# Two heads of sparse attention share one output bank and one transposed bank

## The chip, the core and the metric

The kernel runs on one core of one Trainium2 chip. The metric is the device time of one execution in microseconds (us), the median of several runs. TensorE (PE in the profile, PEld for its weight loads) multiplies, VectorE (DVE) and ScalarE (ACT) do the element work, GpSimd (POOL) and SyncE (SP) mainly issue transfers.

## The reference, cut to what matters

The program is a whole small network on 512 tokens of width 1024: two layers with a linear-recurrence mixer, sparse attention and a gated feed-forward stage, then a third layer with two further attentions, a cross attention and a mixture of 32 experts. The change is in the sparse attention of the first two layers (8 query heads of width 64, 2 key/value groups). Every head adds three attentions with a gate each:

```python
p_cmp = jax.nn.softmax(jnp.where(m_cmp, s, NEG), axis=-1) * m_cmp        # compressed keys
o_cmp = jnp.einsum('bghtn,bngd->btghd', p_cmp.astype(dt), vc)
...
pb = jax.nn.softmax(sb.reshape(B, G, Hg, SLC_QBLOCK, -1), axis=-1)       # selected blocks
return jnp.einsum('bghqns,bgqnsd->bghqd', pb.astype(dt), vg)
...
pw = jax.nn.softmax(jnp.where(mw, sw, NEG), axis=-1)                     # window
return jnp.einsum('bghqk,bkgd->bghqd', pw.astype(dt), vw)
...
o = (gate[..., 0:1] * o_cmp + gate[..., 1:2] * o_slc + gate[..., 2:3] * o_swa)
```

With 512 tokens there are 8 blocks and 16 may be selected, and the window is 512 wide, so the second and the third attention are both plain causal attention over all keys, with keys and values of their own.

## The kernel before, in words

Activations are held transposed, 128 features by 512 tokens to a tile. A product with weights is done in three matmuls of 128x512 (`mm3`, L284 to L286), since weights and activations are each split into a high and a low part. Weights come by `wload` (L266): a DMA on SP's queue into a tile `w`, then the split, ACT writing the high half `wh` (L260) and DVE the low half `wl` (L261). `w` has three buffers, `wh` and `wl` two each.

A layer is a list of steps, `ORDER`, and a list scheduler lays each engine's queue out from the order in which the steps are written and from their dependencies; splits of weights get a higher priority. P, L, A, O are the recurrence, V the values and inputs of the compressed branch, W the compression (96 matmuls of 64x256 with 8 weight tiles `in_c`), K and Q the keys and queries of a group or pair, C the compressed scores and probabilities of a group, H a head, R the two halves of the projection onto the residual. The half R0 needs the recurrence's output alone. Its 96 matmuls (tile `fmm`, weights `fw`, four loads with two buffers, the first held back by `fgate` until the norm of the layer is there) are a filler: the scheduler puts them wherever PE would have nothing else. The diff attention of the third layer uses the same filler lane with eight weight tiles.

A head (`nsa_head`, L801) writes rows 0 to 63 of one PSUM bank `O`. One matmul adds the compressed branch (L807). For each of the other two branches, the scores of the four query blocks (128 queries each, with 128, 256, 384 and 512 keys) come into banks `S` (L525, L526 and a mask, L530). For each block `softmax_rows` takes the row maximum on DVE (L546), a scale (L254), the exponential with row sum on ACT (L551), the reciprocal of the sum (L553), its product with the gate (L254) and the product of the rows with that (L627, by `by_row`), all but the exponential on DVE. `transposed` turns the block triangle of P, ten blocks of 128x128, in three groups of 512, 384 and 256+128 columns (L585, bank `PT`, one buffer) and copies each group to `pth`, every third copy on DVE (L594), the others on ACT (L596). `pv` (L624) adds values times `pth` to `O` with one matmul for each key block, of 512, 384, 256 and 128 columns, with 64 rows of output. The profile shows each of these matmuls as two instructions. At the end of a head ACT copies `O` (L638) and DVE subtracts (L639), for the split of the head's output.

The experts at the end of the program (L1538, L1559) use matmuls with 64 output rows too: neighbouring matmuls write alternately rows 0 to 63 and rows 64 to 127 of a bank.

Of the kernel before, what the change touches and what calls it, by code (L numbers as in the profile page):

```python
# [8 lines left out]
F32 = mybir.dt.float32  # L9
F32R = mybir.dt.float32r  # L10
# [6 lines left out]

PSUM_BUFS = dict(mm=3, fmm=2, tok=4, lev=4, S=3, PT=1, PU=2, O=1, X=2)
CAPS = dict(rT=2, m0=6, sb=1, nl=512, g0=5, w=3, wh=2, wl=2, tmp=6, lf=2, kk=2, qq=2, A=2, eu=3, kf=2, xc=2, rq=4, KH=4, KL=4, T=8, Pc=2,
            P=2, P2=2, pth=3, ptl=3, st=8, stc=2, r4=2, rsx=3, rsy=3, rst=3, hr=2, xtok=2, mh=8, ml=8,  # L20
            hh=22, hl=22, gt=10, sq=2, fw=2, fwh=2, fwl=2, yh=8, yl=8, mgh=8, mgl=8, MKH=4, MKL=4, yt=4, xt=4, ring=20, xgs=2, esg=2, eh=2, ex=2, ehT=2, ey=3, fs=4, fo=4)

ORDER = "P0 L0 A0 V0 O0 O1 W0 K0 Q0 Q1 C0 H0 H1 H2 H3 K1 Q2 Q3 C1 H4 H5 H6 H7 R0 R1"
# [208 lines left out]
class Net:  # L232
# [33 lines left out]
    def wload(self, ap, width, lane=""):  # L266

        nc = self.nc
        w = self.tile([128, 1024], F32, name=lane + "w")
        if lane and self.ngate < 2 * CAPS["fw"]:  # L270
            self.after(w, self.fgate)
            self.ngate += 1
        nc.sync.dma_start(w[:, :width], ap)
        wh = self.tile([128, 1024], F32R, name=lane + "wh")
        wl = self.tile([128, 1024], F32R, name=lane + "wl")
# [53 lines left out]
    def norm(self, src, gain, n=512, pfx="x", spread=True):  # L329
        nc = self.nc  # L330
        xh = self.tile([128, 8, n], F32R, name=pfx + "h")
        xl = self.tile([128, 8, n], F32R, name=pfx + "l")
        acc = self.tile([128, 512], F32, name="acc")
        for k in range(8):
            self.split(xh[:, k, :], xl[:, k, :], src[:, k, :], gain[:, k:k + 1])
            if k == 0:
                nc.scalar.activation(acc[:, :n], src[:, k, :], AF.Square)
            else:
                sq = self.tile([128, 512], F32, name="sq")
                nc.scalar.activation(sq[:, :n], src[:, k, :], AF.Square)  # L340
                self.tt(acc[:, :n], acc[:, :n], sq[:, :n], OP.add)
        nb = n // 128
        rt = self.column(nb)
        ps = self.mmT("X")
        self.sums(ps, acc[:, :n], self.c("ones")[:, 0:1], nb)
        self.rsqrt(rt, ps[:, :nb], 1.0 / D, 1e-6)
        rstd = None
        if spread:
            rstd = self.tile([128, n], F32, name=pfx + "rstd")
# [118 lines left out]
    def nsa_k(self, ps, gain, cos, sin, rtok):  # L468
# [11 lines left out]
        return self.k_stack(x)  # L480
# [9 lines left out]
    def q_stack(self, x, n=512):  # L490

        nc = self.nc
        t0 = self.tile([128, 512], F32R, name="T")
        t1 = self.tile([128, 512], F32R, name="T")
# [147 lines left out]
    def nsa_cv(self, l, xs, rstd, rtok):  # L642
# [11 lines left out]
        v = self.values(256, "nv", False)  # L654
# [24 lines left out]
    def compress(self, l, n):  # L679
# [73 lines left out]
        ckv = self.tile([128, 8, 64], F32, name="ckv")  # L753
# [47 lines left out]
    def nsa_head(self, l, n, h, hi, lo):  # L801

        nc = self.nc
        g = h // 4
        O = self.mmT("O")[:64]
        v = n["v"][0]
        nc.tensor.matmul(O, n["vc"][g][:, h % 4, :], n["pc"][g], start=True, stop=False)  # L807
        for br in range(2):
            Ps = self.p_tiles()
            self.softmax_rows(Ps, lambda qb, w: self.scores(n["q"][h], n["k"][br, g], qb, w, True), n["rq"][h],  # L810
                              n["gate"][:, :, h * 3 + 1 + br])
            pts = self.transposed(Ps, two=False)
            for kc in range(4):
                p, q0 = pts[kc]
                last = br == 1 and kc == 3
                self.pv(O[:, q0:], v[:, kc, br * 128 + g * 64:br * 128 + g * 64 + 64], p, False, last)
        self.out_heads(O, (h % 2) * 64, hi, lo)
# [150 lines left out]
    def layer1(self, l):  # L968
        nc = self.nc
        xs, rstd, rtok = self.norm(self.h, self.p(f"norm_mix{l}"))  # L970
        m = [[self.tile([128, 512], F32R, name=n) for n in ("mh", "ml")] for k in range(8)]
# [3 lines left out]
        def K(g):  # L975
            self.nsa_k_chunk(l, v["n"], xs, rtok, g)

# [6 lines left out]
        def H(h):  # L984
            self.nsa_head(l, v["n"], h, *m[4 + h // 2])
# [276 lines left out]
    def cross(self):  # L1262
# [5 lines left out]
        for i in range(CAPS["xgs"]):  # L1268
            t = self.tile([CAP, D], F32, name=f"xg{i}")
# [81 lines left out]
    def moe(self, out):  # L1351
# [149 lines left out]
        def slot():  # L1501
# [3 lines left out]
            if i < nring:  # L1505
                w = self.tile([128, 2048], F32, name=f"ring{i}")
# [143 lines left out]
def tile_net(ctx, tc, aps, out):  # L1650
# [5 lines left out]
    N.h = N.tile([128, 8, T], F32, name="h")  # L1656
    for k in range(8):
        nc.sync.dma_start(N.h[:, k, :], aps["xT"][:, k, :])
    N.nev = N.nrow = 0
    nc0, np0 = min(_CONST_COLS[n][0] for n in _EARLY), aps["par"].shape[1]  # L1660
    nc2 = aps["const"].shape[1] - nc0
    keep = N.tile([128, nc0 + np0 + 24 + 320 + 192], F32, name="const")
    early = N.tile([128, nc2 + 128 + 768 + 192], F32, name="const2")
# [65 lines left out]
```

## Time and profile before

| | us |
|---|---|
| median of 3 runs | 2526.38 |
| lowest and highest | 2524.33 and 2532.23 |
| the profiled execution, its own time | 2535.04 |
| its span in the profile | 2533.4 |
| PE busy | 2380.5 (94%) |
| DVE busy | 1353.9 (53%) |
| ACT busy | 968.1 (38%) |

The profile is read by stages. In time the stages are: layer one to 770 us, with its heads from about 243 to 400 us; layer two to 1500 us, with its heads from about 985 to 1145 us; the other attentions to about 1985 us; the experts and the tail to the end. The strip of the page that cuts the span into 40 slices shows one slice for each 63 us. "Busy" of PE counts matmul records, whose ends are modelled and overlap, so that a stretch can show 100% and still be packed tighter: what a group of matmuls takes of the engine's time is read from the start of one group to the start of the next.

### The profile page before, as it was taken

How to read it: one execution, taken by the hardware profiler on the slowest of the kernel's cores; microseconds unless marked ns; L12 is line 12 of the kernel's file. 1: busy time of each engine (PE TensorE's matmuls, PEld its weight loads, DVE VectorE, ACT ScalarE, POOL GpSimd, SP SyncE). 2: the span in 40 equal slices, each digit the busy share in tenths (PEclk: the TensorE clock that was granted, in tenths of full speed). 3: DMA queues.
4: the chain of work that ended last, by engine and by line, in shares of the span. 5: the costliest groups of instructions: out<-in, count | busy, mean ns of one | idle time of the engine just before them, and what ended most of it. 6: DMA issues, size and time to landing. Idle time of an engine off the chain costs nothing. (4 is left out here: it accounts for less than half of the span.)

```text
span 2533.4 us, 30397 instructions
## 1 busy us (share of the span) xinstructions
PE 2380.5 (94%) x11422; PEld 1679.7 (66%) x11423; DVE 1353.9 (53%) x3081; ACT 968.1 (38%) x1614; POOL 117.7 (5%) x180
## 2 busy tenths in 40 slices
PE   8999999999999999999999999999999798877776
PEld 6877558888888877558888887777788533222221
DVE  6788876444336778876444338867765511111112
ACT  6544554323226444554232226645443322111111
POOL 0000000000000000000000000000001111111110
PEclk9999999999999999999999999999999799999998
DMA  5123002333333132002333333132235699999997
GB/s 200 44 85 107 17 1 85 98 99 93 100 99 118 35 118 74 9 9 92 94 98 100 93 103 106 48 100 71 91 104 196 234 403 405 404 403 406 408 415 284
DMA packets 83448, 383.15 MB, mean 151 GB/s; under 512 B 12624, under 2 KB 13024, under 8 KB 57952
## 3 DMA queue, kind: packets, MB, share of 16 engines
q1 hardware_dynamic: 77312, 370.65, 41.2%
q0 software_dynamic: 5120, 8.40, 1.0%
q10 hardware_dynamic: 864, 2.10, 0.3%
q8 instruction: 91, 1.49, 0.3%
q14 instruction: 61, 0.50, 0.1%
HBM read 371.66 MB, written 12.59 MB: 152 GB/s over the span
## 5 line engine op out<-in xcount | busy, mean ns | idle before, releaser
L260 ACT ACTIVATE wh<-w 128x1024 fp32r<-128x1024 f32 (+1 forms) x264 | 276.5, 1048 | 615.2 <-PE mm L285 328.9
L284 PE MATMUL mm<-xh,wh 128*128 128x512 f32 x1232 | 490.3, 398 | 10.2 <-ACT wh L260 10.2
L285 PE MATMUL mm<-xl,wh 128*128 128x512 f32 x1232 | 486.2, 395 | 0.0
L286 PE MATMUL mm<-xh,wl 128*128 128x512 f32 x1232 | 484.4, 393 | 0.8 <-DVE wl L261 0.8
L261 DVE TENSOR_TENSOR wl<-w,wh 128x1024 fp32r<-128x1024 f32 (+1 forms) x264 | 320.0, 1212 | 172.8 <-ACT wh L260 171.5
L284 PEld LDWEIGHTS mm<-xh,wh 128*128 128x128 f32 x1232 | 232.7, 189 | 59.9 <-ACT wh L260 10.6
L285 PEld LDWEIGHTS mm<-xl,wh 128*128 128x128 f32 x1232 | 232.9, 189 | 48.2 <-issue 2.9
L286 PEld LDWEIGHTS mm<-xh,wl 128*128 128x128 f32 x1232 | 232.5, 189 | 48.3 <-DVE wl L261 1.4
L254 DVE TENSOR_TENSOR tmp<-mm,xrstd 128x512 f32<-128x512 f32 x104 | 71.7, 691 | 236.0 <-PE mm L286 229.6
L1538 PE MATMUL mm<-ring,ex 128*64 128x512 f32 x512 | 122.9, 613 | 33.2 <-DMA ring<-in_egu_dram 31.5
L1538 PE MATMUL fmm<-ring,ex 128*64 128x512 f32 x512 | 121.5, 606 | 32.4 <-DMA ring<-in_egu_dram 31.7
L284 PE MATMUL mm<-hh,wh 128*128 128x512 f32 x352 | 137.3, 390 | 0.0
L286 PE MATMUL mm<-hh,wl 128*128 128x512 f32 x352 | 137.2, 390 | 0.0
L285 PE MATMUL mm<-hl,wh 128*128 128x512 f32 x352 | 137.2, 390 | 0.0
L1559 PE MATMUL S<-ring,ehT 128*64 128x512 f32 x512 | 123.4, 605 | 12.9 <-DMA ring<-in_ed_dram 9.9
L1538 PEld LDWEIGHTS mm<-ring,ex 128*64 128x64 f32 x512 | 35.6, 139 | 119.1 <-issue 60.6
L1538 PEld LDWEIGHTS fmm<-ring,ex 128*64 128x64 f32 x512 | 35.2, 137 | 116.2 <-issue 60.2
L1525 ACT ACTIVATE xg<-xg,const 64x1024 f32<-64x1024 f32 x32 | 36.6, 1147 | 179.0 <-DMA xg<-x_d,const 179.0
L551 ACT ACTIVATE P<-S,st,const 128x128 f32<-128x128 f32 (+3 forms) x128 | 78.5, 616 | 52.8 <-DVE st L254 42.9
L254 DVE TENSOR_TENSOR eh<-fmm,esg 64x512 f32<-64x512 f32 x16 | 11.1, 693 | 163.3 <-ACT esg L1540 163.3
L254 DVE TENSOR_TENSOR eh<-mm,esg 64x512 f32<-64x512 f32 x16 | 11.1, 693 | 149.6 <-ACT esg L1540 149.5
L546 DVE TENSOR_REDUCE st<-S 128x1 f32<-128x128 f32 (+3 forms) x160 | 76.9, 485 | 26.0 <-PE S L530 25.0
(511 smaller groups left out, 4160.0 us busy)
## 6 DMA issues: line engine op xcount, KB each, us to landing
ring<-in_egu_dram SPq DMA_DIRECT2D x128, 1024.0 KB, 21.7
ring<-in_ed_dram SPq DMA_DIRECT2D x64, 1024.0 KB, 21.4
w<-in_fi_dram SPq DMA_DIRECT2D x88, 512.0 KB, 3.5
w<-in_w_dram SPq DMA_DIRECT2D x48, 512.0 KB, 4.1
w<-in_fo_dram SPq DMA_DIRECT2D x44, 512.0 KB, 3.6
w<-in_c_dram SPq DMA_DIRECT2D x16, 512.0 KB, 3.9
tmp<-tmp SPq DMA_DIRECT2D x80, 64.0 KB, 2.0
fw<-in_wo_dram SPq DMA_DIRECT2D x8, 512.0 KB, 4.6
```

Source lines behind the costliest of these rows:

```text
L254: (eng or self.nc.vector).tensor_tensor(out, a, b, op=op)
L260: nc.scalar.activation(hi, src, AF.Copy)
L261: nc.vector.tensor_tensor(lo, src, hi.bitcast(F32), op=OP.subtract)
L284: nc.tensor.matmul(ps, ah, bh, start=first, stop=False)
L285: nc.tensor.matmul(ps, ah, bl, start=False, stop=False)
L286: nc.tensor.matmul(ps, al, bh, start=False, stop=last)
L546: nc.vector.tensor_reduce(st[:, 0, i:i + 1], S[:, :n], axis=AX.X, op=OP.max, negate=True)
L551: nc.scalar.activation(Ps[q0 + i], S[:, :n], AF.Exp, bias=b, scale=1.0 if scale is None else scale[q0 + i], accum_out=st[:, 1, i:i + 1])
L1525: nc.scalar.activation(xg[:CAP], xg[:CAP], AF.Copy, scale=li_e[2])
L1538: nc.tensor.matmul(ps[r], x[:, k, :], w[:, at:at + 512], start=k == 0, stop=k == 7)
L1559: nc.tensor.matmul(py[r], hT[:, k, :], w[:, at:at + 512], start=k == 0, stop=k == 3)
```

## The change

Two heads go through `nsa_pair` together. Their outputs are rows 0 to 63 and 64 to 127 of one bank. For each branch there are five steps. Each fills one bank `PT` with 512 columns, half from each head, copies it to `pth` in one instruction on ACT, and adds it to `O` with matmuls of 64x256 (64x128 in the fifth step) that stand next to one another for the two heads. The reciprocal and the product with the gate are done once for four rows of statistics (two query blocks of two heads) instead of once for each. `PT` has two buffers instead of one. The output of a pair is copied and subtracted with 128 rows in one instruction each.

The space for this comes from elsewhere: `fw` has one buffer instead of two and waits for the keys of group 0 (`fgate` is set anew after K0); `pth`, `tmp`, `g`, `xc` and `ey` have one fewer; the constants, the residual `h` and a norm's `rstd` are one tile, over parts of which three expert weight buffers lie later; `w` and its halves are one tile each with places taken in turn (same depth).

```diff
-            P=2, P2=2, pth=3, ptl=3, st=8, ...
-            ... fw=2, ... ey=3, ...
+            P=4, P2=2, pth=2, ptl=3, st=8, ...
+            ... fw=1, ... ey=2, ...
-ORDER = "P0 L0 A0 V0 O0 O1 W0 K0 Q0 Q1 C0 H0 H1 H2 H3 K1 Q2 Q3 C1 H4 H5 H6 H7 R0 R1"
+ORDER = "P0 L0 A0 V0 O0 O1 W0 K0 Q0 Q1 C0 H0 H1 K1 Q2 Q3 C1 H2 H3 R0 R1"
-    def nsa_head(self, l, n, h, hi, lo):
...
-        nc.tensor.matmul(O, n["vc"][g][:, h % 4, :], n["pc"][g], start=True, stop=False)
+    def nsa_pair(self, l, n, c, hi, lo):
...
+        heads, rows = (2 * c, 2 * c + 1), (slice(0, 64), slice(64, 128))
+        for h, r in zip(heads, rows):
+            nc.tensor.matmul(O[r], n["vc"][g][:, h % 4, :], n["pc"][g], start=True, stop=False)
+
+        steps = (((0, 1), ((0, (0, 1)),)), ((2, 3), ((0, (2, 3)),)), ((), ((1, (2, 3)),)), ((), ((2, (2, 3)),)), ((), ((1, (1,)), (3, (3,)))))
         for br in range(2):
...
+            Ps = [self.p_tiles() for h in heads]
+            vs = slice(br * 128 + g * 64, br * 128 + g * 64 + 64)
+            for qbs, blocks in steps:
+                if qbs:
+                    st = self.tile([128, 4, 4], F32, name="st")
+                    for i, qb in enumerate(qbs):
+                        w = 128 * (qb + 1)
+                        for j, h in enumerate(heads):
+                            o, scale = slice(2 * j + i, 2 * j + i + 1), n["rq"][h][qb]
+                            S = self.scores(n["q"][h], n["k"][br, g], qb, w, True)
+                            nc.vector.tensor_reduce(st[:, 0, o], S[:, :w], axis=AX.X, op=OP.max, negate=True)
+                            self.tt(st[:, 3, o], st[:, 0, o], scale, OP.mult)
+                            nc.scalar.activation(Ps[j][qb], S[:, :w], AF.Exp, bias=st[:, 3, o], scale=scale, accum_out=st[:, 1, o])
+                    nc.vector.reciprocal(st[:, 2], st[:, 1])
...
+                    self.tt(r, r, gt, OP.mult)
+                    for i, qb in enumerate(qbs):
+                        for j in range(2):
+                            self.by_row(Ps[j][qb], st[:, 2, 2 * j + i:2 * j + i + 1])
+                pt = self.mmT(self.ptn)
...
+                            nc.tensor.transpose(pt[:, at:at + 128], Ps[j][qb][:, kc * 128:kc * 128 + 128], self.c("ident"))
...
+                p = self.tile([128, 512], F32, name="pth")
+                nc.scalar.activation(p, pt, AF.Copy)
+                for kc, j, qs, o in where:
+                    w = 128 * len(qs)
+                    nc.tensor.matmul(O[rows[j], qs[0] * 128:qs[0] * 128 + w], v[:, kc, vs], p[:, o:o + w],
+                                     start=False, stop=br == 1 and kc == 3)
+        nc.scalar.activation(hi, O, AF.Copy)
+        nc.vector.tensor_tensor(lo, O, hi.bitcast(F32), op=OP.subtract)
...
         def K(g):
             self.nsa_k_chunk(l, v["n"], xs, rtok, g)
+            if not g:
+                self.fgate = v["n"]["k"][0, 0][0].bitcast(F32)
```

On PE's queue, in the first layer, at the first values products of a branch, before: `O` is the output bank, `pth` the copied blocks, `nvh` the values, `KH`, `KL` and `T` keys and queries, `PT` the transposed bank.

```order
L585 MATMUL PT_2069<-const_70,P_2017 128x128 x3
L624 MATMUL O_2015<-pth_2067,nvh_996 64x512
L525 MATMUL S_2159<-KH_1759,T_1840 128x128
L526 MATMUL S_2159<-KL_1760,T_1840 128x128
L585 MATMUL PT_2075<-const_70,P_2017 128x128 x3
L624 MATMUL O_2015<-pth_2073,nvh_996 64x384
L530 LDWEIGHTS const2_71
L530 MATMUL S_2159<-const2_71 128x128
L624 MATMUL O_2015<-pth_2079,nvh_996 64x256
L624 MATMUL O_2015<-pth_2079,nvh_996 64x128
```

The same place now (`KK` is the stacked keys):

```order
L854 MATMUL O_1897<-pth_2004,nvh_941 64x256 x2
L854 MATMUL O_1897<-pth_2013,nvh_941 64x128 x4
L848 MATMUL PT_2056<-const_61,P_2019 128x128 x2
L848 MATMUL PT_2056<-const_61,P_2020 128x128 x2
L537 LDWEIGHTS const_61
L537 MATMUL S_2087<-const_61 128x128
L532 MATMUL S_2146<-KK_1652,T_1796 128x128
L533 MATMUL S_2146<-KK_1652,T_1796 128x128
L537 LDWEIGHTS const_61
L537 MATMUL S_2146<-const_61 128x128
L532 MATMUL S_2153<-KK_1652,T_1796 128x128
L854 MATMUL O_1897<-pth_2061,nvh_941 64x256 x2
```

The values products of one head, apart from one another and of unequal width, have become products of two heads that stand together with equal width.

On PE's queue at the end of the compression step W of the first layer, before: `xbh` and `xbl` are the inputs of the compression, the rows with `fmm` are the filler R0, and the rows with `mm<-xh` and `mm<-xl` begin the keys of group 0.

```order
L285 MATMUL mm<-wl,xbh 64x256
L286 MATMUL mm<-wh,xbl 64x256
L284 MATMUL mm<-xh,wh 128x512
L285 MATMUL mm<-xl,wh 128x512
L286 MATMUL fmm<-mh,fwl 128x512
L284 MATMUL fmm<-mh,fwh 128x512
L285 MATMUL fmm<-ml,fwh 128x512
L286 MATMUL mm<-xh,wl 128x512
```

And now (`wx` holds both halves of the weights):

```order
L292 MATMUL mm<-wx,xbh 64x256
L293 MATMUL mm<-wx,xbl 64x256
L291 MATMUL mm<-xh,wx 128x512
L292 MATMUL mm<-xl,wx 128x512
L293 MATMUL mm<-xh,wx 128x512
```

No filler stands here any more, nor among the compression's own 96 matmuls, where 20 stood before; the first `fmm` comes in the step C0.

On SP's queue of the first layer, before, while the recurrence's weights are loaded:

```order
L273 DMA w_410<-in_w3_dram 128x1024
L273 DMA fw_3474<-in_wo_dram 128x1024
L273 DMA fw_3509<-in_wo_dram 128x1024
L273 DMA fw_3544<-in_wo_dram 128x1024
L273 DMA w_446<-in_w3_dram 128x1024
L273 DMA fw_3579<-in_wo_dram 128x1024
```

Now, at the queries (the `tmp` transfers belong to the rotation of a pair's queries):

```order
L440 DMA tmp_1717<-tmp_1696 32x512
L441 DMA tmp_1717<-tmp_1696 32x512
L282 DMA fw_3194<-in_wo_dram 128x1024
L282 DMA w_179<-in_wo_dram 128x1024 x2
L440 DMA tmp_1787<-tmp_1766 32x512
L441 DMA tmp_1787<-tmp_1766 32x512
```

The four loads of `fw` have moved from the recurrence to behind the rotation of keys and of the first queries, and they stand apart, with other transfers queued behind each.

## Rows read from the trace of the kernel before

**Rows 1.** The page, busy tenths of 40 slices of the span.

```profile
PE   8999999999999999999999999999999798877776
DMA  5123002333333132002333333132235699999997
```

**Rows 2.** Stretches: busy us (count) of PE, PEld, DVE, ACT, POOL; PEclk, DMA share, GB/s.

```profile
243.00:400.00 157.00, 153.82 (x732) 92.71 (x731) 128.16 (x502) 86.58 (x208) 2.56 (x2) 1.00 0.06 18
985.00:1145.00 160.00, 156.27 (x741) 94.95 (x740) 127.75 (x518) 84.41 (x206) 2.56 (x2) 0.98 0.06 15
...
2100.00:2200.00 100.00, 82.30 (x415) 29.12 (x412) 12.67 (x21) 21.50 (x29) 13.01 (x14) 0.93 1.02 404
```

**Rows 3.** Timeline of PE in a head: start us, us, instruction, tile, count.

```profile
351.35 1.07 PE L624 MATMUL O<-pth,nvh 128*64 128x512 f32 x2
352.35 0.55 PE L585 MATMUL PT<-const,P 128*128 128x128 f32 x3
352.83 0.86 PE L624 MATMUL O<-pth,nvh 128*64 128x384 f32 x2
353.62 0.50 PE L526 MATMUL S<-KL,T 128*128 128x512 f32 x1
354.05 0.86 PE L624 MATMUL O<-pth,nvh 128*64 128x256 f32 x4
```

**Rows 4.** Timeline of PE at a head's compressed branch.

```profile
251.04 1.07 PE L807 MATMUL O<-pch,ckv 128*64 128x512 f32 x2
252.04 0.55 PE L585 MATMUL PT<-const,P 128*128 128x128 f32 x3
```

**Rows 5.** The experts on PE: timeline, and the group in 2100 to 2200 us (busy, mean ns).

```profile
2202.49 1.94 PE L1538 MATMUL mm<-ring,ex 128*64 128x512 f32 x8
...
L1538 PE MATMUL mm<-ring,ex 128*64 128x512 f32 x96 | 21.9, 597 | 4.2 <-DMA ring<-in_egu_dram 2.8 <-ACT ey L1562 1.3
```

**Rows 6.** Groups on DVE in 243 to 400 us: count, busy us, mean ns, idle before.

```profile
L254 DVE TENSOR_TENSOR st<-st,const 128x1 f32<-128x1 f32 x128 | 17.9, 158 | 0.7
L553 DVE RECIPROCAL st<-st 128x1 f32<-128x1 f32 x64 | 9.7, 158 | 6.1 <-ACT P L551 5.8
L594 DVE COPY pth<-PT 128x384 f32<-128x384 f32 x16 | 8.9, 557 | 6.9 <-PE PT L585 6.3
L627 DVE TENSOR_SCALAR P<-P,st 128x512 f32<-128x512 f32 x16 | 7.7, 482 | 0.2
L639 DVE TENSOR_TENSOR ml<-O,mh 64x512 fp32r<-64x512 f32 x8 | 5.4, 680 | 2.5 <-ACT mh L638 2.5
```

**Rows 7.** Groups on ACT in 243 to 400 us.

```profile
L596 ACT ACTIVATE pth<-PT 128x512 f32<-128x512 f32 x16 | 9.5, 597 | 17.0 <-PE PT L585 15.8 <-PE S L530 1.1
L596 ACT ACTIVATE pth<-PT 128x384 f32<-128x384 f32 x16 | 7.8, 486 | 3.6 <-PE PT L585 3.5
```

**Rows 8.** The compression step, columns as in rows 2 without POOL: filler tile `fmm` alone.

```profile
179.75:196.54 16.79, 5.62 (x20) 3.40 (x20) 0.67 (x1) 0.00 (x0) 1.00 0.62 188
```

**Rows 9.** The same stretch, groups on ACT and DVE.

```profile
L260 ACT ACTIVATE wh<-w 128x1024 fp32r<-128x1024 f32 x8 | 8.5, 1061 | 10.9 <-PE mm L285 5.2 <-PE mm L286 4.8 <-DMA w<-in_c_dram 1.0
L261 DVE TENSOR_TENSOR wl<-w,wh 128x1024 fp32r<-128x1024 f32 x8 | 9.8, 1223 | 2.8 <-ACT wh L260 2.8
```

**Rows 10.** The same stretch, timeline of PE at its first filler.

```profile
179.75 0.28 PE L284 MATMUL mm<-wh,xbh 128*64 128x256 f32 x1
...
181.23 0.40 PE L284 MATMUL fmm<-mh,fwh 128*128 128x512 f32 x1
181.46 0.40 PE L285 MATMUL fmm<-ml,fwh 128*128 128x512 f32 x1
```

**Rows 11.** The page's DMA issues: KB each, median us to landing.

```profile
fw<-in_wo_dram SPq DMA_DIRECT2D x8, 512.0 KB, 4.6
```

**Rows 12.** The filler's loads in the diff attention: first and last start.

```profile
L273 SPq DMA_DIRECT2D fw<-in_bga_dram x4: 328/331/526, 1721.4 to 1747.5; - x4
L273 SPq DMA_DIRECT2D fw<-in_bbr_dram x4: 327/328/526, 1755.0 to 1782.9; - x4
```

More of the change, by code (lines that the diff above doesn't have):

```diff
@@ L268, in wload @@
         nc = self.nc
[L269 to L272, printed above, removed]
+        if lane:
+            w = self.tile([128, 1024], F32, name="fw")
+            if self.ngate < 2 * CAPS["fw"]:
+                self.after(w, self.fgate)
+                self.ngate += 1
+            wh, wl = [self.tile([128, 1024], F32R, name=n) for n in ("fwh", "fwl")]
+        else:
+            i = self.nload
+            self.nload += 1
+            if i == 0:
+                self.places = self.tile([128, 3, 1024], F32, name="w"), self.tile([128, 4, 1024], F32R, name="wx")
+            w, x = self.places[0][:, i % 3], self.places[1]
+            wh, wl = [x[:, j + i % 2] for j in (0, 2)]
         nc.sync.dma_start(w[:, :width], ap)
-        wh = self.tile([128, 1024], F32R, name=lane + "wh")
-        wl = self.tile([128, 1024], F32R, name=lane + "wl")
         with self.tc.high_priority(offset=300):
@@ L348, in norm @@
         if spread:
-            rstd = self.tile([128, n], F32, name=pfx + "rstd")
+            rstd = self.rstd if n == 512 else self.tile([128, n], F32, name=pfx + "rstd")
             pb = self.mmT("X")
@@ L653, in nsa_cv @@
         n["cmp_in"] = cmp_in
-        v = self.values(256, "nv", False)
+        own = self.tile([128, 1536], F32, name="nvh")
+        v = [own[:, :1024].rearrange("p (b n) -> p b n", b=4)]
+        n["own"] = own
         gl, gate = [self.nsa[:, a:a + 96].rearrange("p (b n) -> p b n", b=4) for a in (0, 96)]
@@ L752, in compress @@
         self.tt(xv, xv, y.rearrange(v, g=2)[:, :, :31], OP.add)
-        ckv = self.tile([128, 8, 64], F32, name="ckv")
+        ckv = n["own"][:, 1024:].rearrange("p (a b) -> p a b", a=8)
         ck = self.tile([128, 2, 64], F32R, name="ck")
@@ L808, in nsa_head @@
         for br in range(2):
[L809 to L816, printed above, removed]
@@ L970, in layer1 @@
         xs, rstd, rtok = self.norm(self.h, self.p(f"norm_mix{l}"))
-        m = [[self.tile([128, 512], F32R, name=n) for n in ("mh", "ml")] for k in range(8)]
+        mt = [self.tile([128, 2, 2, 512], F32R, name=f"m{i}") for i in range(8 // 2)]
+        m = [[mt[k // 2][:, k % 2, i] for i in range(2)] for k in range(8)]
         self.fgate, self.ngate = rtok, 0
@@ L984, in H @@
         def H(h):
[L985 removed]
+            self.nsa_pair(l, v["n"], h, *m[4 + h])
         def V(i):
@@ L1268, in cross @@
         for i in range(CAPS["xgs"]):
-            t = self.tile([CAP, D], F32, name=f"xg{i}")
+            if i == 0:
+                both = self.tile([128, 2, D], F32, name="xg")
+            t = both[:CAP, i]
             nc.gpsimd.tensor_copy(t.rearrange("p (a b) -> p a b", a=2), self.h[:CAP, 6:8, :])
```

49 lines of the change are left out of this document (32 added, 17 removed).

## The prediction

> **What bounds the kernel now.** First the strip of 40 slices [rows 1]. PE stands at nine tenths in all but the first of some 31 slices, about 1985 us, while the DMA row stays low; then the DMA row goes to nine and PE falls. So until the experts start PE's queue sets the time, and from there the weights' transfers do. Time saved on PE before the experts moves the experts forward as a whole and is kept. The experts themselves have a DMA share of 1.02 [rows 2], and nothing in the change makes them move fewer bytes.
>
> Then the stretches of the heads [rows 2]: of 157 and 160 us PE is busy 153.8 and 156.3, DVE 128 and 128, ACT 87 and 84. PE is the bound, DVE has a fifth of its time left, ACT almost half. But busy PE is not PE at its peak, so next the timeline, from the start of a group to the start of the next.
>
> **Part 1, the values products.** In a head, the group of 512 columns takes 352.35 - 351.35 = 1.00 us, that of 384 columns 353.62 - 352.83 = 0.79, and the third (256 and 128 columns, together 384) has the duration of the second, 0.86, so I give it 0.79 too [rows 3]. A head-branch takes 2.58 us, a pair's branch 5.16. From the first two, 128 columns more cost 0.21 us, that is 1.64 ns a column, and 512 x 1.64 = 0.84, so that a group costs 0.16 us besides its columns. The product of the compressed branch takes 252.04 - 251.04 = 1.00 [rows 4].
>
> What two products in two halves of the bank take is seen in the experts, which write 64 rows each in turn: eight instructions of 512 columns, four logical products, span 1.94 us, and one lasts 0.597 [rows 5]. If two run at a time there are four slots, (1.94 - 0.597) / 3 = 0.448 us apart, 0.875 ns a column. Run one by one, eight instructions at 0.82 ns a column (half of 1.64) would take some 3.4 us. So two do run at once. A logical product is two instructions, so a pair of products takes two slots: 1.75 ns a column for both heads where they now take 3.28.
>
> After the change a pair's branch has 4 x 256 + 2 x 128 = 1280 columns for each head, as before, in five groups: 1280 x 1.75 ns = 2.24 us plus 5 x 0.16 = 3.04 us, against 5.16. That is 2.12 us x 16 (4 pairs, 2 branches, 2 layers) = 33.9 us. The compressed product of a pair takes 512 x 1.75 ns + 0.16 = 1.06 for 2.00, 0.94 x 8 = 7.5 us. Together **-41.4 us**. The rows show this for 512 columns and the same stationary width, 64; for 256 and 128 columns no row shows it, so the other end is no overlap at all. Then only groups are saved: 96 + 16 before, 80 + 8 after, 24 x 0.16 = -3.8 us. I take the first, as the experts have the same form.
>
> **Part 2, statistics and copies.** Per layer DVE loses 48 of 64 reciprocals and 48 gate products at 158 ns each, 15.2 us, the 16 copies, 8.9, and 4 of 8 output subtractions at 680 ns, 2.7 [rows 6]: 27 us, so 128 becomes 101. ACT has 40 copies of 512 columns at 597 ns, 23.9 us, where it had 9.5 + 7.8 [rows 7], and four output copies fewer (by the same price, 2.4): 87 becomes 91. On DVE and ACT the sum is nothing, since both stay below the some 135 us that PE then needs; their cover is PE's own work, and it gets thinner.
>
> The cost is waiting. A group of four rows of statistics is done when its fourth exponential is; then come reciprocal and gate (2 x 0.158), four row products (up to 0.482 each, [rows 6]) and the copy (0.597): 2.84 us until the first values product may start. Behind that product on PE's queue stand scores and transposes of the next steps, as the order shows; they can't pass it. Before, the same chain per block was shorter and PE hardly waited (3 of 157 us without a matmul). The two `PT` banks and the scores of the next step put ahead of the product cover some of it. Ends: 0, and 2.84 us once for each of 16 pair-branches, 45 us. I take one copy uncovered in each, 16 x 0.6 = **+10 us**, nearer to the low end, because the row of before shows PE almost without waits at DVE's higher load.
>
> Against this edit stands a rule: the Trainium skill, TensorEngine Tiling (Array Packing), Performance Considerations, says that tiling speeds up TensorE but not the emptying of PSUM, which may then become the bound, and asks for both ScalarE and VectorE on it. The change puts it all on ACT. By throughput the rows don't bear it out (24 us of copies in some 135); by latency it is the rival of the exposed chain below.
>
> **Part 3, the filler leaves the compression.** In the compression PE waits for split weights: of 16.8 us the 20 fillers fill a part [rows 8]. Its own 13 matmuls from 179.75 to 181.23 are 0.114 us apart, so 96 take 10.9; a filler takes 0.23 to its successor [rows 10], 20 take 4.7. Now the first `fw` waits for the keys of group 0, so the fillers run later at full price. The compression does not stay as long, though: a split buffer comes free when PE has finished its tile, 12 x 0.114 = 1.37 us, then ACT takes 1.06 and DVE 1.22 [rows 9], 3.65 us for one of two buffers, 8 x 3.65 / 2 = 14.6 us. It gains 2.2 and the fillers cost 4.7 elsewhere: 2.5 us a layer, **+5 us**. Ends: 0 (the fillers meet gaps that nothing else fills) and 9.4 (the stage stays as long). SP's queue is passed too: the `fw` loads (4.6 us to landing, [rows 11]) now stand ahead of rotation transfers and residual weights, and the second waits for the first one's split. I price that in the next part.
>
> **Part 4, one `fw` buffer.** A tile then needs 4.6 us of transfer and 1.06 + 1.22 of splits one after the other, 6.9 us, while its 24 matmuls take 5.6. In the diff attention eight loads start from 1721.4 to 1782.9 [rows 12], 8.8 us apart, slower than 6.9. So the cover is the attention between the fillers. Ends 0 and 8 x 1.3 = 10; I take **+2 us**.
>
> **Part 5, the rest.** One buffer fewer for `tmp`, `g`, `xc`, `pth` and `ey`, and one tile for constants and residual, add no instruction. A wait that one of them causes would be on DVE or ACT, which have slack while PE works, and in the experts the transfers hide it. Nothing; if that cover is gone, it is one more copy time here and there.
>
> **The sum.** -41.4 + 10 + 5 + 2 = -24.4 us. Made against the profiled execution's own time, 2535.0, it gives 2510.6; that execution lies 8.7 above the median of the runs, and the steps counted here are all before the experts, so I take the difference over unchanged: 2526.4 - 24.4 = **2502 us**.
>
> **The rivals.**
> *All of it is kept:* no wait in the heads and no loss in the compression, -41.4 + 2: **2487**. For it: DVE is relieved by 27 us a layer, and `PT` is doubled. Against: the static queue and the fuller statistics.
> *The chain is half exposed:* 1.42 us in each pair-branch, 22.7 in place of the 10: -41.4 + 22.7 + 7 = -11.7, **2515**. For it: each pair-branch has two such groups, and only the next scores and the filler lie between a group's exponentials and its product. Against: the same as for the forecast.
> *Slower, the chain is wholly exposed:* each pair-branch pays the 2.84 us once on PE's queue, between the last exponential of a group of four and its first values product. -41.4 + 45.4 + 7 = +11, **2537**. It decides from 2.6 us a pair-branch, (41.4 + 7.6 - 7) / 16, on. For it: the product stands ahead of the next scores. Against: the filler (some 72 matmuls a layer in the heads) stands in such places.
> *The change doesn't do what it says:* the halves don't run at once at 256 columns. -3.8 + 17 = +13, **2540**. Against: the experts' rows.
>
> **How the numbers follow.** Forecast 0.50, with a range of its own of 2491 to 2513; all kept 0.17; half exposed 0.17; wholly exposed 0.09; no overlap 0.07. About 0.3% (7.6 us) is what a measurement of this kernel can tell from no change. Faster by more: 0.50 + 0.17 and 0.10 of the half exposed, 0.77; within: 0.08, the rest of the half exposed and a little of the slower ones; slower: 0.15. The range leaves out the two slower cases and the low edge of the second, 0.2 together: 2483 to 2530.
>
> **What would show it.** Right: in the heads a group of two 256-column products is 0.6 us from start to start; the stretch of a layer's heads is 18 to 22 us shorter; DVE busy there falls by 27 us and ACT rises by 4; the compression shows PE gaps and no `fmm`; the experts begin some 24 us earlier and last as long. Wrong: values products whose starts are as far apart as now (part 1); PE waits in the heads for DVE's row products or ACT's copies of more than 1 us a pair-branch (part 2); a compression without gaps (part 3); PE waits for `fwh` in the diff attention (part 4); a longer stretch of experts (part 5). A clock below its high level would do it too: the heads have a granted clock of 1.00 and 0.98, and the experts, where PE is busy 82%, 0.93 [rows 2], so that waits on PE may cost more than their length.

## The result

| | median us | runs | ratio to before, 95% interval |
|---|---|---|---|
| before | 2529.16 (2524.33 to 2532.23) | 4 | |
| changed | 2504.85 (2497.8 to 2506.43) | 4 | 0.9894 [0.9877, 0.9911] |
| changed, second group of runs | 2500.52 (2497.47 to 2502.13), before 2530.31 there | 4 | 0.9878 [0.9863, 0.9893] |

The change makes the kernel faster by 24.3 us in the first group, 29.8 in the second. The forecast was 24.4 us and 2502 us. The total is as forecast; of its terms the largest held, and the others missed in both directions. Of the four executions of the kernel with one `PT` bank (below) one took 3288.71 us at a granted clock of 0.65, and its median is that of the other three.

The two profiled executions lie 37.2 us apart (spans of 2533.4 and 2496.2), since the one of before is 5.9 us above its median and the one of after 7.1 below. Stages can be compared in profiled executions alone, so the stages below sum to 37, or to 33 with the second profiled execution of the changed kernel (2500.2). The remainder to the medians can't be put to a stage.

Two groups of instructions bound the stages in both kernels: the compression's matmuls (`xbh`) and the last product of the feed-forward stage (`hh`). This is the view of one tile's instructions, one window to a layer; columns are duration in ns (least, median, most), then first and last start. Before:

```profile
L284 PE MATMUL mm<-wh,xbh x32: 274/277/334, 179.7 to 196.3; 128*64 128x256 f32 x32
L284 PE MATMUL mm<-hh,wh x176: 389/389/395, 640.5 to 759.7; 128*128 128x512 f32 x176
L284 PE MATMUL mm<-wh,xbh x32: 276/276/334, 928.8 to 945.4; 128*64 128x256 f32 x32
L284 PE MATMUL mm<-hh,wh x176: 389/389/398, 1392.7 to 1512.5; 128*128 128x512 f32 x176
```

After:

```profile
L291 PE MATMUL mm<-wx,xbh x32: 276/276/334, 177.0 to 193.7; 128*64 128x256 f32 x32
L291 PE MATMUL mm<-hh,wx x176: 389/389/389, 623.7 to 742.7; 128*128 128x512 f32 x176
L291 PE MATMUL mm<-wx,xbh x32: 276/276/334, 912.1 to 928.5; 128*64 128x256 f32 x32
L291 PE MATMUL mm<-hh,wx x176: 389/389/389, 1356.5 to 1475.5; 128*128 128x512 f32 x176
```

From the compression's last matmul to the first of `hh` lie keys, queries, heads, residual and the first feed-forward half; of these only the heads and the fillers differ. I call it the heads' stretch. It was 444.2 and 447.3 us, and is 430.0 and 428.0: 14.2 and 19.3 us less. The compression is as long as before, 16.7 and 16.4 us between these starts. It begins 2.7 us earlier in the first layer, and from the first layer's `hh` to the second's compression nothing changes (288.3 and 288.4). Whatever the heads give is kept until the experts, as the forecast had it: they started at 2019.7 us and start at 1981.4.

**The values products.** Timeline of PE after (start, duration, instruction, tile, count), three places with the row behind each:

```profile
327.94 0.65 PE L854 MATMUL O<-pth,nvh 128*64 128x256 f32 x4
328.52 0.98 PE L848 MATMUL PT<-const,P 128*128 128x128 f32 x7
...
344.23 1.08 PE L818 MATMUL O<-pch,nvh 128*64 128x512 f32 x4
345.14 0.60 PE L854 MATMUL O<-pth,nvh 128*64 128x256 f32 x4
...
349.33 1.08 PE L854 MATMUL O<-pth,nvh 128*64 128x256 f32 x8
350.35 1.09 PE L848 MATMUL PT<-const,P 128*128 128x128 f32 x8
```

They answer [rows 3, 4]. A step of two products of 256 columns takes 0.58 us from start to start, two steps together 1.02, where 384 columns of one head took 0.79. The compressed products of a pair take 0.91, where one head's took 1.00.

**The heads by engine**, 139 us of the first layer (columns as in [rows 2]), and the groups on DVE and ACT that answer [rows 6, 7]:

```profile
243.00:382.00 139.00, 132.86 (x807) 92.63 (x806) 107.55 (x385) 88.94 (x213) 2.56 (x2) 0.96 0.08 23
```

```profile
L835 DVE RECIPROCAL st<-st 128x4 f32<-128x4 f32 x16 | 2.8, 175 | 7.0 <-ACT P L834 6.9
L254 DVE TENSOR_TENSOR st<-st,const 128x1 f32<-128x1 f32 x64 | 9.2, 153 | 0.3
L254 DVE TENSOR_TENSOR st<-st,const 128x4 f32<-128x4 f32 x16 | 2.6, 162 | 0.2
L851 ACT ACTIVATE pth<-PT 128x512 f32<-128x512 f32 x40 | 22.4, 596 | 18.0 <-PE PT L848 17.8
```

Reciprocals went from 9.7 to 2.8 us, the products of statistics from 17.9 to 11.8 (9.2 for the scales, 2.6 for the gates in fours), DVE's copies are gone, and DVE's busy time went from 128.2 to 107.6: 20.6 us less, where the forecast said 27. PE is without a matmul for 6.1 of 139 us, where it was 3.2 of 157, and its granted clock is 0.96 where it was 1.00. Over the whole heads' stretch PE is without a matmul for 8.6 and 8.2 us, where it was 4.1 and 4.3.

**The compression** in both layers, columns the same:

```profile
177.00:193.80 16.80, 12.95 (x98) 10.82 (x97) 13.35 (x17) 10.76 (x12) 0.00 (x0) 1.00 0.59 185
912.10:928.65 16.55, 13.02 (x98) 10.84 (x97) 13.24 (x17) 10.77 (x12) 0.00 (x0) 1.00 0.57 185
```

PE now has a matmul in it for 12.95 of 16.8 us. The 20 fillers left gaps, and the stage did not get shorter by them.

### The profile page after: what moved, and what is told of

Its sections match the earlier page's. It is cut to its first block, busy times and chain, and to the rows that moved or that the text cites. A ratio compares the mean times of both kernels' runs of the same rounds, so it can differ in the third digit from the quotient of the medians.

```text
span 2496.2 us, 30418 instructions
## 1 busy us (share of the span) xinstructions
PE 2320.9 (93%) x11550; PEld 1665.8 (67%) x11551; DVE 1316.6 (53%) x2849; ACT 973.7 (39%) x1622; POOL 118.7 (5%) x174
## 5 line engine op out<-in xcount | busy, mean ns | idle before, releaser
L260 ACT ACTIVATE wx<-w 128x1024 fp32r<-128x1024 f32 (+1 forms) x264 | 276.6, 1048 | 663.2 <-PE mm L292 355.8
L291 PE MATMUL mm<-xh,wx 128*128 128x512 f32 x1232 | 489.0, 397 | 11.6 <-ACT wx L260 10.5
L293 PE MATMUL mm<-xh,wx 128*128 128x512 f32 x1232 | 484.3, 393 | 1.4 <-DVE wx L261 1.4
L292 PE MATMUL mm<-xl,wx 128*128 128x512 f32 x1232 | 483.8, 393 | 0.0
L261 DVE TENSOR_TENSOR wx<-w,wx 128x1024 fp32r<-128x1024 f32 (+1 forms) x264 | 320.7, 1215 | 169.1 <-ACT wx L260 168.4
L291 PEld LDWEIGHTS mm<-xh,wx 128*128 128x128 f32 x1232 | 232.1, 188 | 61.0 <-ACT wx L260 10.7
L293 PEld LDWEIGHTS mm<-xh,wx 128*128 128x128 f32 x1232 | 231.7, 188 | 51.4 <-DVE wx L261 4.6
L292 PEld LDWEIGHTS mm<-xl,wx 128*128 128x128 f32 x1232 | 231.9, 188 | 48.2 <-issue 2.9
L254 DVE TENSOR_TENSOR tmp<-mm,const 128x512 f32<-128x512 f32 x104 | 71.7, 691 | 239.9 <-PE mm L293 233.1
L291 PE MATMUL mm<-hh,wx 128*128 128x512 f32 x352 | 136.9, 389 | 0.0
L292 PE MATMUL mm<-hl,wx 128*128 128x512 f32 x352 | 136.9, 389 | 0.0
L293 PE MATMUL mm<-hh,wx 128*128 128x512 f32 x352 | 136.9, 389 | 0.0
L254 POOL TENSOR_TENSOR tmp<-tmp,const 128x512 f32<-128x512 f32 x20 | 30.5, 1523 | 1208.2 <-DMA tmp<-tmp 979.2
## 6 DMA issues: line engine op xcount, KB each, us to landing
ring<-in_ed_dram SPq DMA_DIRECT2D x55, 1024.0 KB, 21.5
```

The lines of the kernel that those rows point to most:

```text
L254: (eng or self.nc.vector).tensor_tensor(out, a, b, op=op)
L260: nc.scalar.activation(hi, src, AF.Copy)
L261: nc.vector.tensor_tensor(lo, src, hi.bitcast(F32), op=OP.subtract)
L291: nc.tensor.matmul(ps, ah, bh, start=first, stop=False)
L292: nc.tensor.matmul(ps, ah, bl, start=False, stop=False)
L293: nc.tensor.matmul(ps, al, bh, start=False, stop=last)
```

## The experiments

The theory after the first profile: the packing of two products is worth the 41 us that the rows of before gave, the fillers that left the compression are paid in full, and what the heads wait for is small. The rivals: the gain is DVE's relief and the fuller statistics, not the packing; and the fillers are worth nothing in either place. Stretches are taken from the same two groups as above, the first layer's and the second's; times are medians, "start" is the first matmul of the compression.

| run | us | ratio, 95% | start | heads' stretch |
|---|---|---|---|---|
| before (profile) | 2529 to 2531 | 1 | 179.7 | 444.2, 447.3 |
| changed (first profile) | 2504.85 | 0.9894 | 177.0 | 430.0, 428.0 |
| changed, again | 2500.52 | 0.9878 [0.9863, 0.9893] | 177.2 | 428.8, 429.1 |
| fillers back in the compression | 2515.13 | 0.9942 [0.9928, 0.9955] | 185.3 | 433.9, 432.9 |
| one `PT` bank | 2513.39 | 0.9926 [0.9906, 0.9947] | 182.0 | 433.3, 433.7 |
| both heads in one half | 2545.44 | 1.0061 [1.0045, 1.0076] | 177.2 | 452.0, 455.2 |
| before, filler late | 2536.1 | 1.0026 [1.0016, 1.0036] | 175.2 | 450.3, 450.3 |
| statistics for each block | 2495.93 | 0.9863 [0.9845, 0.9881] | 177.0 | 431.2, 426.9 |
| copies shared with DVE | 2519.97 | 0.9962 [0.9946, 0.9977] | 181.1 | 437.6, 437.1 |
| keys ahead of the compression | 2520.5 | 0.9957 [0.9943, 0.9971] | 187.2 | (other stages in it) |
| three `PT` banks | 2517.61 | 0.9951 [0.9939, 0.9964] | 181.3 | 435.7, 435.5 |
| each block, three banks | 2523.67 | 0.9971 [0.9959, 0.9982] | 181.8 | 437.9, 445.3 |
| each block, two outputs | 2504.24 | 0.9895 [0.9881, 0.9909] | 181.6 | 432.3, 430.2 |
| two `fw` buffers | 2519.13 | 0.9953 [0.9938, 0.9969] | 177.5 | 431.9, 432.3 |

### The changed kernel again

> The changed kernel as it is, as the yardstick of this group of runs. Both theories: ratio to the kernel before 0.9894 within 0.002, some 24 to 27 us faster; in the trace the compression step of 16.8 us with no filler in it.

As expected in time, and a little faster than the first time. The compression has no filler, but lasts 16.8 us in neither layer: 16.5 in the second and 18.3 in the first, at a granted clock of 0.91. The heads' stretch agrees within 1.2 us, so a difference of 3 us in that stretch is more than the scatter of these two profiles. But an edit also makes the scheduler order PE's queue anew. Two edits below that leave every instruction of the heads as it is (three `PT` banks, two `fw` buffers) lengthen the stretch by 3 to 7 us a layer, so that a difference of this size need not come from what an edit does to the instructions.

### The packing, taken away

The control, with one bank:

```diff
-PSUM_BUFS = dict(mm=3, fmm=2, tok=4, lev=4, S=3, PT=2, PU=2, O=1, X=2)
+PSUM_BUFS = dict(mm=3, fmm=2, tok=4, lev=4, S=3, PT=1, PU=2, O=1, X=2)
-... eu=3, ...
+... eu=2, ...
```

> The changed kernel with one PT bank instead of two (and two buffers instead of three for eu in the recurrence, for space). Theory (part 2 of the prediction: the second bank covers the copies): each of 80 steps waits up to a part of the 0.6 us copy, 5 to 20 us slower than the changed kernel. Rival (other work on PE's queue covers the copies anyway): within 3 us. It is also the control for the next run, which has one PT bank for the same reason.

The run without packing has the same and this besides:

```diff
-PSUM_BUFS = dict(mm=3, fmm=2, tok=4, lev=4, S=3, PT=1, PU=2, O=1, X=2)
+PSUM_BUFS = dict(mm=3, fmm=2, tok=4, lev=4, S=3, PT=1, PU=2, O=2, X=2)
-        O = self.mmT("O")
+        Os = [self.mmT("O")[:64] for j in range(2)]
...
-                    nc.tensor.matmul(O[rows[j], qs[0] * 128:qs[0] * 128 + w], v[:, kc, vs], p[:, o:o + w],
+                    nc.tensor.matmul(Os[j][:, qs[0] * 128:qs[0] * 128 + w], v[:, kc, vs], p[:, o:o + w],
...
+        for O, r in zip(Os, rows):
+            nc.scalar.activation(hi[r], O, AF.Copy)
+            nc.vector.tensor_tensor(lo[r], O, hi[r].bitcast(F32), op=OP.subtract)
```

> The run before, and the two heads of a pair write rows 0 to 63 of two output banks instead of two halves of one: the same products in the same order, none of them in different halves; two output copies and subtractions a pair again. Theory (the gain is that products in two halves run at once): values products take 41 us more over both layers, so 30 to 42 us slower than the run before, and slower than the kernel before by some 10 us. Rival (the gain comes from fewer instructions on DVE and from the pairing of the statistics): within 10 us of the run before.

The products are the same and only their rows differ, but the order of the queue is not quite the same: of the 96 fillers of a layer 48 stand in the last pair and behind it, where the control has none. Timeline of PE in the run with both heads in one half:

```profile
344.62 1.08 PE L854 MATMUL O<-pth,nvh 128*64 128x256 f32 x4
345.63 0.66 PE L848 MATMUL PT<-const,P 128*128 128x128 f32 x4
...
355.48 1.93 PE L818 MATMUL O<-pch,nvh 128*64 128x512 f32 x4
357.25 1.03 PE L854 MATMUL O<-pth,nvh 128*64 128x256 f32 x4
```

The four instructions that take 0.58 us packed take 345.63 - 344.62 = 1.01, and the compressed products 1.77 in place of 0.91. The heads' stretch is 18.7 and 21.5 us longer than the control's, 40.2 together; the forecast's term was 41.4. The values products alone, each counted from its start to the start of PE's next matmul, show the same without the rest of the queue: 56.7 us over both stretches in the control, 96.6 here, 39.9 more. The medians differ by 32.1, in the range expected; the control begins its compression 4.8 us later (of which more below). Without packing the changed kernel is slower than before. So the packing is more than the whole gain, and the rival falls.

The control's own heads' stretch is 4.5 and 4.6 us longer than in the second profile of the changed kernel. The waits of PE in its heads have the row that the second bank shortens; in the changed kernel the same wait is 1.0 us. So some 2 us a layer are the copies, and the rest of the 4.5 can be the new order:

```profile
PE O L854 <- ACT pth L851: 3.2, 5, 0.7
```

### The fillers, put back

```diff
-            if not g:
-                self.fgate = v["n"]["k"][0, 0][0].bitcast(F32)
...
             v["n"] = self.nsa_cv(l, xs, rstd, rtok)
+            self.fgate = v["n"]["own"]
```

> The changed kernel, except that the first load of fw waits for the values step V instead of the keys of group 0, so that 23 fillers stand in the compression again (20 of them within its 16.8 us). Theory (the compression lasts as long without them, so each filler moved out is paid in full: 20 x 0.235 us, 4.7 us a layer): 9 us faster than the changed kernel, ratio to before 0.986, the stretch of a layer's heads 4.7 us shorter, the compression again 16.8 us long. Rival (the moved fillers only fill waits that the heads have anyway): within 3 us of the changed kernel.

Neither came. The compression has its fillers back and is as long as ever (16.6 us, all of it with matmuls):

```profile
185.30:201.90 16.60, 16.60 (x117) 14.18 (x116) 13.86 (x18) 10.79 (x12) 0.00 (x0) 1.00 0.60 185
```

But the heads, with 20 fillers fewer, did not get 4.7 us shorter; they got some 4 us longer. One place is the last pair of a layer. Waits of PE there in the timeline (the wait and its releaser stand in brackets), each with the matmul before it, in this run and then in the changed kernel:

```profile
365.99 0.23 PE L537 MATMUL S<-const 128*128 128x128 bf16 x1
369.12 2.18 PE L848 MATMUL PT<-const,P 128*128 128x128 f32 x8 [2.90 <-DVE P L634]
```

```profile
357.34 0.39 PE L293 MATMUL mm<-m,wx 128*128 128x512 f32 x1
358.45 0.41 PE L848 MATMUL PT<-const,P 128*128 128x128 f32 x2 [0.72 <-DVE P L634]
```

PE waits 2.9 us for the row products of a group of four, with nothing else to do. In the changed kernel nine products of the residual projection R1 (`mm<-m`) stand between the last scores of the layer and these transposes, in both layers; here none stands there, and no filler stands there in either kernel. Over both heads' stretches PE is without a matmul for 24.3 us here, 16.9 in the changed kernel, and the clock takes 3.4 us more (what the clock takes is the length of a stretch times what its granted clock lacks to 1.00, as in the last section). The rest of the loss isn't settled. Of the 8 us by which the compression begins later, 5.1 are the clock (below); for the others, the loads of `fw` stand ahead of the compression's weights on SP's queue, which may be the cause.

The same move by itself, in the kernel before (`fgate` set after K0; `hh=22` made 21):

```diff
             self.nsa_k_chunk(l, v["n"], xs, rtok, g)
+            if not g:
+                self.fgate = v["n"]["k"][0, 0][0].bitcast(F32)
```

> The kernel before with one edit of the change alone: the filler's weights wait for the keys of group 0 (and one buffer fewer for the high half of the feed-forward values, for space). Theory (single heads keep PE busy by themselves and have no waits for a filler to fill; the paired heads have them): the compression stays 16.8 us long with some 5 us of gaps, the heads get the fillers on top, so 9 us slower than the kernel before, ratio 1.0037. Rival 1 (part 3 of the prediction: the compression gets shorter without fillers): 5 us slower. Rival 2 (the filler costs nothing wherever it stands): within 3 us of the kernel before.

The heads' stretch is 6.1 and 3.0 us longer, 9.1 together, as the theory had it (2 x 4.7). The compression did not get shorter, 17.8 and 16.4 us between its first and last starts (the clock takes 3.4 us of the first). The median is 0.26% up, less than these 9 us. In the profile the compression of the first layer begins 4.5 us earlier, with the `fw` loads gone from the recurrence, and the stretch between the layers is 3.7 us shorter, 3.4 of them clock that the profile of before lost there. Both halves matter: the late filler costs the heads some 4.5 us a layer where PE is full, and the earlier start comes with its transfers and splits gone from the stage ahead.

### Statistics, copies, banks and buffers

Reciprocal and gate for each block again:

```diff
-                    nc.vector.reciprocal(st[:, 2], st[:, 1])
...
-                    self.tt(r, r, gt, OP.mult)
                     for i, qb in enumerate(qbs):
                         for j in range(2):
+                            o = slice(2 * j + i, 2 * j + i + 1)
+                            nc.vector.reciprocal(st[:, 2, o], st[:, 1, o])
+                            self.tt(st[:, 2, o], st[:, 2, o], n["gate"][:, qb, 6 * c + 3 * j + 1 + br:6 * c + 3 * j + 2 + br], OP.mult)
```

> The changed kernel with reciprocal and gate product for each row block again (48 more of each a layer, 15 us of DVE). Theory A (part 2 of the prediction: a group of four is done only with its fourth exponential, and PE waits for it): up to 10 us faster than the changed kernel, the waits of transposes for P shorter. Theory B (the two DVE instructions more lie on the same chain and cost as much as the early start gains): within 4 us. Theory C (DVE is near its limit in the heads): 8 us or more slower.

Theory B: the stretch is 431.2 and 426.9, and the interval of the ratio overlaps that of the changed kernel. The statistics in fours are worth nothing that can be measured, though they take this much off DVE (64 reciprocals in the heads of this run, 16 in the changed kernel's):

```profile
L838 DVE RECIPROCAL st<-st 128x1 f32<-128x1 f32 x64 | 9.8, 156 | 2.2 <-ACT P L834 1.9
```

Every third copy on DVE (and `eu=2`):

```diff
-                nc.scalar.activation(p, pt, AF.Copy)
+                self.nev = (self.nev + 1) % 3
+                if self.nev < 1:
+                    nc.vector.tensor_copy(p, pt)
+                else:
+                    nc.scalar.activation(p, pt, AF.Copy)
```

> The changed kernel with every third copy of PT on DVE again (and two buffers instead of three for eu in the recurrence, for space; the heads alone are compared). Theory (by throughput no engine is the bound of the heads): the stretch of a layer's heads within 2 us of the changed kernel's. Rival (the emptying of PSUM on ACT alone has become the bound): the stretch 3 us or more shorter. The other way is open too: DVE has the row products of the chain, a copy of 0.6 us between them makes the stretch up to 5 us longer.

The other way, and more than expected: the stretch is 8.8 and 8.0 us longer than in the second profile of the changed kernel. So giving copies back to DVE gains nothing. Not all of these 17 us need be the copies, since three banks, which move no copy, cost 13 (below), and 5 us of the 17 are the clock. Again PE waits for row products in the last pair, 3.53 us, with no product of R1 between the last scores and that wait:

```profile
368.98 0.41 PE L848 MATMUL PT<-const,P 128*128 128x128 f32 x2 [3.53 <-DVE P L634]
```

Keys ahead of the compression:

```diff
-ORDER = "P0 L0 A0 V0 O0 O1 W0 K0 Q0 Q1 C0 H0 H1 K1 Q2 Q3 C1 H2 H3 R0 R1"
+ORDER = "P0 L0 A0 V0 O0 O1 K0 W0 Q0 Q1 C0 H0 H1 K1 Q2 Q3 C1 H2 H3 R0 R1"
```

> The changed kernel with the keys of group 0 (K0) written ahead of the compression (W0), so that the filler, gated by these keys, may stand in the last third of the compression. Theory (fillers are worth as much in the heads as in the compression): within 4 us of the changed kernel. Rival (PE's gaps in the compression, 5 us a layer, are lost time that a filler there wins back): 5 to 9 us faster.

Slower than both expected. The compression's first matmul to its last is now 27.5 and 28.1 us; PE waits in its middle for the split of its second input, which stands behind the keys on DVE:

```profile
PE mm L293 <- DVE xbl L261: 5.8, 1, 5.8
```

Three banks, then the same with each block's own statistics, and each block's own statistics with two banks `PT` and two output banks (`O=2`):

```diff
-PSUM_BUFS = dict(mm=3, fmm=2, tok=4, lev=4, S=3, PT=2, PU=2, O=1, X=2)
+PSUM_BUFS = dict(mm=3, fmm=2, tok=4, lev=4, S=3, PT=3, PU=2, O=1, X=2)
```

> The changed kernel with three PT banks. Theory (the second bank shortened each layer's heads by 4 to 5 us since it hides the copy; a third hides what is left of it): the heads up to 2 us a layer shorter, 0 to 4 us faster than the changed kernel's 2500.5 of the first group. Rival (what is left are the statistics, not the banks): within 2 us, with the waits of products for pth unchanged at some 1 us.

> Statistics for each row block again, and three PT banks. Theory (with each block's own statistics P comes in smaller pieces, so that a third bank lets PE transpose ahead): 3 us or more faster than statistics for each block alone, 2495.9. Rival: within 3 us of it.

> Statistics for each row block again, and two output banks, so that a pair's first product need not wait until the pair before is copied out. Theory (PE waits 0.7 us there by the trace, four times a layer at most): 1 to 3 us faster than statistics for each block alone, 2495.9. Rival (filler and scores cover that wait): within 2 us. Beside the others it is a third look at statistics for each block.

None is faster, and for none of the three did the theory or the rival come. Three banks lengthen the heads by 7 us a layer (5 of the 13 us over both layers are the clock), and the wait in the last pair is there once more, again with no product of R1 between the last scores and it:

```profile
370.45 1.97 PE L848 MATMUL PT<-const,P 128*128 128x128 f32 x8 [2.90 <-DVE P L634]
```

A third bank changes no instruction, only what the scheduler may put where. With each block's own statistics the third bank costs 6.7 us in the first layer and 18.4 in the second. Of the 18.4 some 12 are the clock, which takes 15.4 us of that stretch (granted 0.97), and 3.4 with two banks (0.99). Two output banks gain nothing.

Two buffers for `fw` (and `eu=2`):

```diff
-... fw=1, ...
+... fw=2, ...
```

> The changed kernel with two fw buffers again (and two for eu in the recurrence, for space). Theory (part 4 of the prediction: the single buffer costs 2 us, mostly in the diff attention): the stretch from the end of the second layer to the experts 1 to 3 us shorter. Rival (the attention between the fillers hides the loads): that stretch within 1 us of the changed kernel's.

Neither expectation came. From the second layer's first `hh` matmul to the experts it takes 632.5 us, and 624.9 in the changed kernel (both profiles), 627.0 before. So the single buffer costs nothing there; the stretch with one is 2.1 us shorter than before.

No version beats the changed kernel clear of its interval. Statistics for each block (0.9863 [0.9845, 0.9881]) equals it (0.9878 [0.9863, 0.9893]).

## Why the prediction was right, and where it was not

**The bound** held: PE's time before the experts is kept as a whole.

**Part 1, -41.4: right.** Taking the packing away costs 40.2, and the values products, counted as above, take 43.5 us less than before over both stretches. A step of 256 columns was put at 2 x 256 x 0.875 ns + 0.16 = 0.61 us and takes 0.58; the doubt about widths under 512 is settled.

**Part 2, +10: mis-sized, too high.** The two profiles put the heads' stretch at -33.5 and -33.6. Take from that -40.2 for the packing and +9.4 for fillers that moved in, and about -3 remain for all else in the heads, waits included. Counted in PE's own time, from each start to the next, the first profile agrees: values products -43.5, fillers +12.9, all else -2.9. The waits themselves did come, at about the size that was forecast: PE is without a matmul for 8.4 us more than before, and the clock takes 5.1 us more. What the term missed is that the rest of PE's work in the heads became cheaper by about as much; what made it so isn't settled. The second bank shortens the wait for copies by some 2 us a layer, as the term had it. The sign of 18 to 22 us less in a layer's heads was larger than the terms allow, since 41.4 less 10 gives 15.7 a layer even before fillers move in; 14.2 to 19.3 were measured.

The rule of the Trainium skill that was weighed there, TensorEngine Tiling (Array Packing), Performance Considerations, would share the emptying of PSUM between ScalarE and VectorE; here the run that does so has heads 8 to 9 us a layer longer. That DVE carries the chain from maximum to row products while ACT had idle time is a likely reason, but the run changes the order of the queue too.

The slower rival priced an exposed chain at 2.84 us for each pair-branch. Where a wait of PE is exposed it is 2.90 us in four experiments (fillers back, keys first, three banks, two `fw` buffers). It happens once a layer there, in the last pair, and not in every pair-branch; in the changed kernel that wait is 0.72. That the two figures agree is luck: the rival's sum runs from the last exponential through four row products and the copy, and the wait runs from the last scores through maximum, exponential and reciprocal to the first row product. So the size was near, and the place and the path were wrong.

**Part 3, +5: the size was off, from a wrong step.** "The compression does not stay as long" was the step that failed: between its first and last starts it takes 16.2 us or more with or without fillers, in both kernels, so the cost is the upper end, 9.4 (9.1 in the kernel before). The working took the release of a split buffer as the limit; no run settles which step of the supply is. What the term did not see is that putting the fillers back gains nothing in paired heads.

**Part 4, +2:** nothing measurable; the stretch is 2.1 us shorter. **Part 5, nothing:** the first layer's compression begins 2.7 us earlier. The kernel before with the late filler alone shows 4.5, so it comes with part 3's move, as a gain that the forecast left out: the `fw` loads and splits no longer stand in the recurrence. In the second layer no such gain shows.

**The sum.** By stages after minus before is -2.7 (start), 0 (compression), -33.5 (heads' stretches), -2.1 (to the experts), +1.1 (experts and tail), in all -37 with rounding, against -24.4. By medians it is -24 to -30. So the point forecast agrees with the medians, while the stages of single executions moved more: the term of the waits was too high by some 13, that of the fillers too low by 4, and two gains of 3 and 4 were not seen. Together the terms were off by some 13 us, mostly in one direction, and did not cancel. That the medians meet the point forecast is in part luck: the two profiled executions, one above its median and one below, lie 13 us further apart than the medians, and no stage can be named for that.

**Chances.** By the medians the forecast itself came (-24.3 and -29.8 for -24.4); by the stages of single executions it is nearer to "all of it is kept".

## What to carry to other kernels

Products with 64 output rows that a kernel issues one after the other into the same rows are the first thing to look for: in two halves of a bank, next to one another, they take 0.58 us in place of 1.01, and the price can be read beforehand from any other stage that already does it. When two units of work are merged, look at the last merged unit, where no scores of a next one follow. In the changed kernel nine products of the residual projection stand between its last scores and its transposes and PE waits 0.72 us; in five experiments with statistics in fours nothing stands there and it waits 2.9 to 3.5. In a static queue even a buffer more can move such work away, so the order is to be read again after each edit, and a small difference between two versions can be the order and not the edit.

## What was not expected of the hardware

TensorE's granted clock falls in stages that look full. Columns as above, the same 20 us of before and after:

```profile
260.00:280.00 20.00, 19.31 (x90) 9.65 (x88) 17.37 (x74) 11.90 (x32) 1.27 (x1) 1.00 0.06 15
```

```profile
260.00:280.00 20.00, 18.98 (x120) 12.23 (x120) 14.71 (x53) 15.00 (x37) 1.27 (x1) 0.87 0.09 25
```

PE is busy for all but 1 us in both, yet the granted clock is 1.00 and 0.87: for about a quarter of the stretch it was at 1.2 GHz instead of 2.4, which is 20 x 0.13 = 2.6 us of work lost. Over the first layer's heads the changed kernel loses some 5 us so (139 x 0.04), and before lost none. The same shows at other places: in the run with the fillers back the clock is 0.85 between 60 and 80 us,

```profile
60.00:80.00 20.00, 18.75 (x98) 16.16 (x97) 13.40 (x21) 10.73 (x12) 0.00 (x0) 0.85 0.15 52
```

where the changed kernel has 1.00 with the same 18.75 us busy. Seven experiments have this dip (0.83 to 0.85) and begin the compression at 181.1 us or later; the others, both profiles of the changed kernel and before have none, and begin it between 175.2 and 179.7. It is some 3 us of the later start. Two of the seven have an edit in the recurrence (`eu=2`), but so have two runs without the dip. PE's records ahead of it don't tell the runs apart either: from 60 to 73 us PE is without a matmul for 1.25 to 1.30 us in the seven, and for 1.25 in the changed kernel. What decides it, in a kernel or in one execution of it, stays open; executions of one kernel differ in the mean granted clock too, from 0.973 to 0.982 with three banks.
